# One layer of a hybrid backbone: where decays, context products, head weights and the last splits are placed

## The chip, the cores and the metric

The kernel runs on one core of a Trainium2 chip. A core has TensorE (PE: matrix products into the accumulation memory PSUM, from a stationary operand that a weight load brings in, PEld), VectorE (DVE), ScalarE (ACT: copies, casts, activation functions), GpSimd (POOL) and SyncE (SP: starts transfers). The engines run side by side; each takes its own instructions in order, and semaphores tie them together. The metric is the device time of one execution in microseconds (us). The kernel before takes 1752.54 us, the median of three runs (1750.49 to 1753.95).

## The reference

One layer of a diffusion backbone over 1024 latent tokens (a 16 x 64 grid) and 256 context tokens, of width 1024, all in fp32:

```python
hx = _modulate(_rmsnorm(x, norm1_g[l]), sh1, sc1)        # shifts and scales from c @ w_ada
hc = _modulate(_rmsnorm(ctx, norm1_g[l]), csh1, csc1)
... = jnp.split(hx @ w_in[l], IN_OFFSETS, axis=-1)       # q, k, v of both branches, gates
o_na = _na_latent(grid(xq), grid(xk), grid(xv), kc_na, vc_na, na_rpb[l])
o_ret_c, s_f, s_b = _bi_retention(qc_r, kc_r, vc_r, lg_f, lg_b, s_zero, s_zero)
o_ret_x, _, _ = _bi_retention(q_r, k_r, _heads(xrv, RET_HEADS), lg_f, lg_b, s_f, s_b)
o_ret = _ret_output(o_ret_x, xrg)
x = x + g1 * _merge(o_na, o_ret, xga, xgb, w_proj_na[l], w_proj_ret[l], w_out[l])
x = x + g2 * _conv_ffn(hx2, w_up[l], conv_w[l], conv_b[l], w_down[l])
return _rmsnorm(x, final_norm_g)
```

`_na_latent` is neighbourhood attention (8 heads of 64, window 8 x 16) over local keys and all context keys in one softmax. `_bi_retention` is a chunked linear recurrence in both directions (4 heads, chunks of 128, a log decay `lg` for each head and direction). Its decays inside a chunk are `exp(lg * (pos + 1))`, `exp(lg * (L - 1 - pos))`, and for a whole chunk `exp(lg * L)`; they depend on the position and the head alone.

## The kernel before, in words

**Arithmetic.** Each fp32 operand of a large product is split into a high part, which ScalarE makes with a cast (L88), and a low part, which VectorE makes with a subtraction (L89). Three matmuls, high x high, high x low and low x high, make up one product (`chain` at L105 to L114, `mm3` at L122 to L125, `open3` at L1384 to L1387). A weight tile of 128 x 512 comes by DMA into one of three `raw` buffers (L93), and its split goes into one of six `wc` places, or into a place given by the caller (`wload`). A raw buffer is free for the next load when both halves of its split are done.

**Order.** Each engine's queue follows from when the program is built. Most code is put in order by a program with modelled durations, which takes the earliest written instruction that is ready; it may draw an instruction far ahead of its place in the text if nothing gates it. Code under `tc.manual_schedule()` keeps its written order on every engine, while instructions from outside may be put in between. A tile that reuses memory waits for the readers of the tile that had it before.

**Start (hand-ordered, up to L1010).** Loads, norms, transposes and modulation of the tokens; the products for the first pair of attention heads gather in PSUM tiles `c` (three for each half of the tokens, `first_mm`). At its end stand: `decays(0)` to `decays(3)` (L596 to L604: 24 exponentials of 128 x 1 on ScalarE) and `dec_scale` on POOL (L607); the release of the start's buffers; the evictions `ev_hi` and `ev_lo` of `c` into queries `qS`, keys `kH` and `kL`, and values `vT`; the next pair's query weights, whose second half goes into `place` (ScalarE L635, VectorE L638); products with them (`next_mm`), in the two-buffer PSUM tag `mm`, and their evictions; and last the products of the context tokens with the key and value weights, `ctx_mm(1)` and `ctx_mm(2)`:

```python
    def ctx_mm(t):
        m = mt[0, t, 2] = mm_tile()
        mm_a(m[:, :C], first[t], hcs(0), hcs(1))
```

The SBUF tile `ex`, which holds the exponents of the decays, lies in the start's pool `s0`. PSUM has eight banks. In the start they hold two `tp` and the six `c`; then two go to `mm` and six to the attention's pool `pna` (tags `sl`, `sc`, and `pt` with two buffers).

**Attention.** 32 units (4 pairs of heads x 8 query blocks), each with scores, softmax, transposes and products with the values; further projections fill TensorE between them (`piece`). The ScalarE exponentials are at L484 and L485.

**Retention.** For each head h, `Head(h)` loads eight weight tiles: for head 0 six into `wc` and two into `wx` (six places of their own), for the others 0 to 3 into `wc` and 4 to 7 into `wx`. `front(i)` then makes ten blocks (two of context, eight of the grid) with eight products each, in the order of the weights. `state(i)` makes the running state from `kz` (keys times decay), and the mixing of the head before runs in between.

**Down projection (the end).** Seven products by a Strassen-like scheme, each a sum over eleven weight blocks j, into four PSUM banks for four token blocks. In the last product seven blocks run under `steps(6, ...)`; the last four (`tl`) are split before a hand-ordered part, where TensorE works bank by bank. `finish` (L1938 to L1946) scales a block's output: small POOL operations, one ScalarE and one VectorE instruction, two DMAs from SP. Of the last four blocks of the sixth product, two are finished in the ordered part and two behind the first bank of the hand-ordered part.

Of the kernel before, what the change touches and what calls it, by code (L numbers as in the profile page):

```python
# [8 lines left out]
F32 = mybir.dt.float32  # L9
F32R = mybir.dt.float32r  # L10
AF = mybir.ActivationFunctionType
ALU = mybir.AluOpType
# [4 lines left out]
P = 128  # L17
# [23 lines left out]
def tile_hybrid_layer(ctx, tc: tile.TileContext, io, dbg=None):  # L41
# [24 lines left out]

    cpool = sb("const", "left")
    edge = sb("edge", "right")
    tick = cpool.tile([P, 24], F32, name="pad")[:, 0:1]
    edge.tile([P, 24], F32, name="pad")  # L70

    def const(name, shape):
# [26 lines left out]
    def wload(src, lo_eng=None, into=None):  # L99
        raw = rawload(src)  # L100
        wc = into if into is not None else wtile()
        split(wc[:, 0], wc[:, 1], raw, lo_eng)
        return wc
# [18 lines left out]
    def mm3(out, ah, al, bh, bl, first, last):  # L122
        pe.matmul(out, ah, bh, start=first, stop=False)  # L123
        pe.matmul(out, ah, bl, start=False, stop=False)  # L124
        pe.matmul(out, al, bh, start=False, stop=last)  # L125
# [218 lines left out]
    def mm_tile():  # L344
        return pmm.tile([P, 512], F32, tag="mm", bufs=2, name="mm")
# [184 lines left out]
    def ada_load():  # L530
        w = na.tile([P, D], F32, tag="aw", bufs=2, name="aw")
        sync.dma_start(w, io["w_ada2"][len(ada2)])
        ada2.append(w)
# [56 lines left out]

    def load_ex():
        cst["lg"] = const("lg", [P, 2, RH])
        cst["ex"] = s0.tile([P, 5], F32, name="ex")
        sync.dma_start(cst["ex"], io["expo"])

    def decays(h):  # L596
        lg, ex = cst["lg"], cst["ex"]
        f, b = lg[:, 0, h : h + 1], lg[:, 1, h : h + 1]
        act.activation(dec[:, h, 0:1], ex[:, 0:1], AF.Exp, scale=f)
        act.activation(dec[:, h, 1:2], ex[:, 1:2], AF.Exp, scale=b)  # L600
        act.activation(dec[:, h, 2:3], ex[:, 2:3], AF.Exp, scale=f)
        act.activation(dec[:, h, 3:4], ex[:, 3:4], AF.Exp, scale=b)
        act.activation(dec[:, h, 4:5], ex[:, 4:5], AF.Exp, scale=f)
        act.activation(dec[:, h, 5:6], ex[:, 4:5], AF.Exp, scale=b)  # L604

    def dec_scale():
        pool.tensor_scalar(dec[:, :, 0:2], dec[:, :, 0:2], RKS, None, ALU.mult)  # L607


    pairs, mt, gens = [], {}, {}  # L610
    blocks = {(0, t): first[t] for t in range(3)}
# [38 lines left out]
        pairs[1].evac_lo(0, half, h, mt[1, 0, half])  # L650

    def ctx_mm(t):
        m = mt[0, t, 2] = mm_tile()
        mm_a(m[:, :C], first[t], hcs(0), hcs(1))


# [1 line left out]
    with tc.manual_schedule():  # L658
# [297 lines left out]
        first_mm(0, 7)  # L956
        ctx_l(6)
        ctx_l(7)
        decays(0)
        decays(1)  # L960
        decays(2)
        decays(3)
        first_mm(1, 7)
        dec_scale()
        next_load(1)
        s0.release()
        na = sb("na", "right")
# [91 lines left out]
    for i in range(NPAIR * NJ + 2):  # L1059
        live = i < NPAIR * NJ  # L1060
        u1 = us[i - 1] if 1 <= i <= NPAIR * NJ else None
        u2 = us[i - 2] if i >= 2 else None
        if i == 0:
            ada_load()
            ada_load()
        for n in (0, 1) if i == 1 else (i,) if 1 < i < 32 else ():
            ada_col2(n)
        if u1:
            if u1.j == 0:
                u1.pair.values()  # L1070
            u1.transp(0)
        piece()
        if u1:
            u1.transp(1)
        if live:
            pair = pairs[i // NJ]
            if i % NJ == 0 and i:
                pair.load_bias()
            us.append(Unit(pair, i % NJ))
            us[i].scores()  # L1080
        if u2:
            u2.output()
        if u1:
            u1.values()
            puts(gate_sums, u1.st[:, 14:15], 1)
        piece()
        piece()
# [26 lines left out]
    class Head:  # L1114
        def __init__(self, h):
            self.h = h
            fwd = h % 2 == 0
            self.order = list(range(NTB)) if fwd else list(range(NTB - 1, -1, -1))
            self.back = self.order[::-1]
            self.ci = 0 if fwd else 1  # L1120
            self.oi = 1 - self.ci
            self.wr = []
            for kb in range(KB):
                t = rt.tile([P, 2, 512], F32R, tag="wx", bufs=6, name="wx") if kb >= (KH if h else 6) else None
                self.wr.append(wload(io["w_ret"][h, kb], into=t))
            self.init = [rt.tile([P, DV], F32, tag=f"init{i}", bufs=2, name=f"init{i}") for i in range(2)]
            self.v, self.qk, self.sts, self.dss, self.r0 = {}, {}, {}, {}, {}
            self.sts[self.order[0]] = self.init[self.ci]
            self.run = self.init[self.oi]
            self.o, self.A, self.Q = {}, {}, {}  # L1130
# [4 lines left out]
        def front(self, i):  # L1135

            src, tb = (hcp, i) if i < NCB else (hxp, self.order[i - NCB])
            c0 = P if i < NCB else 0
            m = mm_tile()
            for kb in range(KB):  # L1140
                xh, xl = src(0, kb, tb * P, P), src(1, kb, tb * P, P)
                w = self.wr[kb]
                mm3(m[:, c0:512], xh, xl, w[:, 0, c0:512], w[:, 1, c0:512], kb == 0, kb == KB - 1)
                if kb in (2, 5):
                    yield
            vtag = f"c{i}" if i < NCB else tb
            self.v[i] = v = rt.tile([P, 2, DV], F32R, tag=f"v{vtag}", bufs=1, name="v")
            act.copy(v[:, 0], m[:, 256:512])
            vec.tensor_tensor(v[:, 1], m[:, 256:512], v[:, 0].bitcast(F32), ALU.subtract)
            r0 = rt.tile([P, 2, 2, 2, 32], F32, tag="r0", bufs=2, name="r0")  # L1150
            self.r0[i] = r0f = r0.rearrange("p q a t i -> p q (a t i)")
            if i < NCB:
                act.copy(r0f[:, 1], m[:, P : 2 * P])
                return
            r1 = rt.tile([P, 2, 2, 2, 32], F32, tag="r1", bufs=2, name="r1")
            mv = m[:, 0:256].rearrange("p (q a t i) -> p q a t i", q=2, a=2, t=2)
            for a, ti in ((0, tb), (1, NTB)):
                cs = cosT[:, ti, 0].unsqueeze(1).unsqueeze(1).to_broadcast([P, 2, 2, 32])
# [756 lines left out]
    def gs(dh):  # L1915
        return slice(dh * 512, dh * 512 + 512)
# [21 lines left out]
    def finish(tb, dh):  # L1938
        s, ts = ssf[:, tb], slice(tb * P, (tb + 1) * P)
        pool.tensor_scalar(s[:, 3:4], s[:, dh : dh + 1], 1.0 / D, s[:, 2:3], ALU.mult, ALU.add)  # L1940
        pool.tensor_tensor(s[:, 4:5], s[:, 3:4], mhalf[:, 0:1], ALU.pow)
        z0, z1 = part[tb, 1 - dh], part[tb, dh]
        act.activation(z0, z0, AF.Copy, scale=s[:, 4:5])
        vec.scalar_tensor_tensor(z1, z1, s[:, 4:5], fg[:, gs(dh)], ALU.mult, ALU.mult)
        sync.dma_start(io["out"][ts, gs(1 - dh)], z0)
        sync.dma_start(io["out"][ts, gs(dh)], z1)  # L1946

    stream = Stream([(j, c) for p in DOWN for j in range(NH) for c in p], 8)
# [37 lines left out]
    for b in range(QB):  # L1986
        tb = QB + b
        x, z = rows_of(tb, 0), dw_tile("z", 6)
        part[tb, 0] = z
        vec.tensor_tensor(z, u2[b], banks[1][b], ALU.subtract)  # L1990
        pool.tensor_tensor(z, z, gate2[:, gs(0)], ALU.mult)
        pool.tensor_tensor(z, z, x, ALU.add)
        square(tb, 0, x)
        if b < QB - 2:
            finish(tb, 0)

    steps(6, range(NH - NL), False, False)
    tl = [operands(6, j) for j in range(NH - NL, NH)]
    with tc.manual_schedule():
        for b in range(QB):  # L2000
            ts = slice(b * P, (b + 1) * P)
            for i, (a, w) in enumerate(tl):
                open3(banks[0][b], a[:, 0, ts], a[:, 1, ts], w[:, 0], w[:, 1], False, i == NL - 1)
            if b == 0:
                for tb in (NTB - 2, NTB - 1):
                    finish(tb, 0)
            z, junk = dw_tile("z", 6), dw_tile("xr", 4)
            part[b, 1] = z
            vec.tensor_tensor(z, banks[0][b], gate2[:, gs(1)], ALU.mult)
            vec.tensor_tensor(z, p1[b], z, ALU.subtract)  # L2010
            square(b, 1, junk)
            if b:
                finish(b - 1, 1)
        finish(QB - 1, 1)
# [110 lines left out]
```

## Time and profile before

| what | us |
|---|---|
| three runs, median (lowest to highest) | 1752.54 (1750.49 to 1753.95) |
| the profiled execution, its own time | 1753.51 |
| its span in the profile | 1751.7 |
| VectorE busy, of the span | 1224.6 |
| ScalarE busy, of the span | 852.3 |
| TensorE busy from 112 to 383 (attention) | 270.58 of 271 |

The profile shows one execution. Times count from the start of its span. A row of the timeline gives the start, the duration, the engine (SPq is SP's queue of transfers), the line of the kernel, the operation, what is written from what, and the shapes; x2 at its end means that two such instructions follow each other, and brackets give the idle time of the engine before it and what ended it. A row of the table of stretches gives the length, then the busy time and number of instructions of PE, PEld, DVE, ACT and POOL, then the granted TensorE clock as a share of full speed, the busy share of the DMA engines and their GB/s. The end of a matmul is modelled, so matmuls overlap in the rows; their starts tell the pace.

### The profile page before, as it was taken

How to read it: one execution, taken by the hardware profiler on the slowest of the kernel's cores; microseconds unless marked ns; L12 is line 12 of the kernel's file. 1: busy time of each engine (PE TensorE's matmuls, PEld its weight loads, DVE VectorE, ACT ScalarE, POOL GpSimd, SP SyncE). 2: the span in 40 equal slices, each digit the busy share in tenths (PEclk: the TensorE clock that was granted, in tenths of full speed). 3: DMA queues.
4: the chain of work that ended last, by engine and by line, in shares of the span. 5: the costliest groups of instructions: out<-in, count | busy, mean ns of one | idle time of the engine just before them, and what ended most of it. 6: DMA issues, size and time to landing. Idle time of an engine off the chain costs nothing.

```text
span 1751.7 us, 25084 instructions
## 1 busy us (share of the span) xinstructions
PE 1724.2 (98%) x8405; PEld 1426.8 (81%) x8405; DVE 1224.6 (70%) x2454; ACT 852.3 (49%) x1826; POOL 537.6 (31%) x703
## 2 busy tenths in 40 slices
PE   8999999999999999999999999999999999999997
PEld 4688888888888888888888888788888888888886
DVE  4777788765776766765554556876888889856755
ACT  5666666653443534553444323544444444545444
POOL 1000001002333344513222211012566657421444
PEclk9999999999999999999999999999999999999999
DMA  9144455541322313578876666767666676998754
GB/s 345 63 152 148 126 145 160 177 119 35 103 71 62 88 40 97 159 250 271 272 228 235 194 198 191 253 218 224 189 182 169 188 199 173 256 315 289 242 162 162
DMA packets 141362, 313.02 MB, mean 179 GB/s; under 512 B 19025, under 2 KB 31473, under 8 KB 135025
## 3 DMA queue, kind: packets, MB, share of 16 engines
q1 hardware_dynamic: 117040, 230.66, 39.1%
q0 software_dynamic: 12032, 70.27, 18.0%
q10 hardware_dynamic: 12160, 10.49, 1.8%
q8 instruction: 66, 1.08, 0.3%
q14 instruction: 64, 0.52, 0.1%
HBM read 250.78 MB, written 121.91 MB: 213 GB/s over the span
## 4 chain that ended last, share of the span: by engine, by line
PE 50%; issue 6%; DVE 4%; DMA 4%; POOL 4%; ACT 2%; SPq 0%; POOLq 0%; ACTq 0%; DVEq 0%
PE u L1387 28%; PE pr L114 2%; PE pr L112 2%; PE pr L113 2%; DMA ur<-d_a 2%; PE mm L125 1%; PE mm L123 1%; PE mm L124 1%; PE om L125 1%; PE om L123 1%; PE om L124 1%; DMA d_a<-at 1%; PE pn L113 1%; PE pn L112 1%; PE pn L114 1%
## 5 line engine op out<-in xcount | busy, mean ns | idle before, releaser
L1387 PE MATMUL u<-T,wc 128*128 128x512 f32 x960 | 225.1, 390 | 0.5 <-ACT pu L1421 0.4
L1387 PE MATMUL y<-wc,ahl 128*128 128x512 f32 x924 | 210.4, 389 | 2.1 <-DVE wc L89 2.1
L1387 PEld LDWEIGHTS u<-T,wc 128*128 128x128 f32 x960 | 179.6, 188 | 40.1 <-ACT pu L1421 2.7
L1387 PEld LDWEIGHTS y<-wc,ahl 128*128 128x128 f32 x924 | 173.3, 188 | 38.9 <-DVE wc L89 2.9
L89 DVE TENSOR_TENSOR wc<-ur,wc 128x512 fp32r<-128x512 f32 x161 | 117.1, 730 | 60.2 <-ACT wc L88 58.3
L88 ACT CAST wc<-ur 128x512 fp32r<-128x512 f32 x161 | 99.8, 622 | 118.8 <-PE u L1387 71.4
L113 PE MATMUL mm<-low,wc 128*128 128x512 f32 (+1 forms) x328 | 124.8, 381 | 0.0
L1387 PE MATMUL u<-h2a,wc 128*128 128x512 f32 x480 | 112.8, 390 | 0.1
L112 PE MATMUL mm<-hx,wc 128*128 128x512 f32 x264 | 107.5, 407 | 0.2 <-ACT wc L635 0.2
L1387 PEld LDWEIGHTS u<-h2a,wc 128*128 128x128 f32 x480 | 89.9, 188 | 19.7 <-issue 0.8
L114 PE MATMUL mm<-hx,wc 128*128 128x512 f32 x264 | 105.7, 400 | 0.0
L1387 PE MATMUL u<-hxT,wc 128*128 128x512 f32 x384 | 89.6, 389 | 0.0
L584 POOL COPY pad<-pu 128x1 f32<-128x1 f32 x54 | 36.9, 683 | 160.1 <-DVE pu L1424 117.0
L1387 PEld LDWEIGHTS u<-hxT,wc 128*128 128x128 f32 x384 | 72.1, 188 | 15.0
L584 POOL COPY pad<-st 128x1 f32<-128x1 f32 x32 | 5.9, 185 | 250.7 <-DVE st L487 250.7
L89 DVE TENSOR_TENSOR wc<-raw,wc 128x512 fp32r<-128x512 f32 x86 | 61.9, 722 | 17.3 <-ACT wc L88 17.3
L88 ACT CAST wc<-raw 128x512 fp32r<-128x512 f32 x86 | 53.1, 623 | 39.4 <-PE u L1387 7.4
L88 ACT CAST wc<-s 128x512 fp32r<-128x512 f32 x56 | 34.9, 624 | 69.9 <-PE u L1387 67.7
L125 PE MATMUL mm<-wc,low 128*128 128x512 f32 (+1 forms) x180 | 68.5, 381 | 0.0
L113 PEld LDWEIGHTS mm<-low,wc 128*128 128x128 f32 x328 | 62.9, 192 | 6.8
L1182 ACT ACTIVATE kz<-r,dec 128x128 fp32r<-128x128 f32 x72 | 27.8, 402 | 71.9 <-POOL r L1163 71.5
L1387 PE MATMUL u<-hx,wc 128*128 128x512 f32 x192 | 62.0, 390 | 0.0
(407 smaller groups left out, 4763.4 us busy)
## 6 DMA issues: line engine op xcount, KB each, us to landing
d_a<-at SPq DMA_DIRECT2D x77, 256.0 KB, 5.6
ur<-d_a SPq DMA_DIRECT2D x77, 256.0 KB, 5.3
ur<-in_w_up SPq DMA_DIRECT2D x74, 256.0 KB, 6.7
d_w<-in_w_down POOLq DMA_DIRECT2D x66, 256.0 KB, 7.2
aw<-in_w_ada SPq DMA_DIRECT2D x32, 512.0 KB, 4.1
d_a<-d_a POOLq DMA_DIRECT2D x44, 256.0 KB, 7.5
ur<-d_w SPq DMA_DIRECT2D x44, 256.0 KB, 3.9
d_s<-in_w_up POOLq DMA_DIRECT2D x36, 256.0 KB, 6.1
```

The source lines that it names most:

```text
L88: act.copy(hi, src)
L89: (lo_eng or vec).tensor_tensor(lo, src, hi.bitcast(F32), ALU.subtract)
L112: pe.matmul(out, wh, xh, start=k == 0, stop=False)
L113: pe.matmul(out, wh, xl, start=False, stop=False)
L114: pe.matmul(out, wl, xh, start=False, stop=k == n - 1)
L123: pe.matmul(out, ah, bh, start=first, stop=False)
L124: pe.matmul(out, ah, bl, start=False, stop=False)
L125: pe.matmul(out, al, bh, start=False, stop=last)
L584: late(pool.tensor_copy(tick, src))
L1182: act.activation(kz[:, d, 0], k, AF.Copy, scale=self.dec(d))
L1387: pe.matmul(out, a, b, start=first and n == 0, stop=last and n == 2, skip_group_check=True)
```

## The change

Four edits. (1) The 24 exponentials become six multiplications of `lg` by a column of `ex` on VectorE, each for all heads, and one exponential over the whole of `dec` on ScalarE; they and the scaling on POOL are called in the attention's loop, at unit 8. `ex` moves to the constant pool, whose padding tile shrinks from 24 to 16 columns. (2) The context products go into the attention's `pt` banks. (3) Heads 1 to 3 begin each block with weights 4 to 7 and end with 0 to 3, and the weights are loaded in an order that goes with that. (4) The splits of the last four blocks of the down projection move into the hand-ordered part; three blocks instead of two are finished behind its first bank; the last block's first output goes out from ScalarE's queue.

```diff
-    tick = cpool.tile([P, 24], F32, name="pad")[:, 0:1]
+    tick = cpool.tile([P, 16], F32, name="pad")[:, 0:1]
+    ex = cpool.tile([P, 5], F32, name="ex")
...
-        cst["ex"] = s0.tile([P, 5], F32, name="ex")
-        sync.dma_start(cst["ex"], io["expo"])
-
-    def decays(h):
-        lg, ex = cst["lg"], cst["ex"]
-        f, b = lg[:, 0, h : h + 1], lg[:, 1, h : h + 1]
-        act.activation(dec[:, h, 0:1], ex[:, 0:1], AF.Exp, scale=f)
...
-    def dec_scale():
+        sync.dma_start(ex, io["expo"])
+
+    def decays():
+        for k, e in enumerate((0, 1, 2, 3, 4, 4)):
+            vec.tensor_scalar(dec[:, :, k], lg[:, k % 2], ex[:, e : e + 1], None, ALU.mult)
+        act.activation(dec, dec, AF.Exp)
         pool.tensor_scalar(dec[:, :, 0:2], dec[:, :, 0:2], RKS, None, ALU.mult)
...
     def ctx_mm(t):
-        m = mt[0, t, 2] = mm_tile()
+        m = mt[0, t, 2] = pna.tile([P, 512], F32, tag="pt", bufs=2, name="cm")
         mm_a(m[:, :C], first[t], hcs(0), hcs(1))
...
-        decays(0)
-        decays(1)
-        decays(2)
-        decays(3)
         first_mm(1, 7)
-        dec_scale()
         next_load(1)
...
+        if i == 8:
+            decays()
...
-            self.wr = []
-            for kb in range(KB):
+            self.kbs = (*range(KH, KB), *range(KH)) if h else range(KB)
+            self.wr = {}
+            for kb in (4, 5, 0, 1, 6, 7, 2, 3) if h > 1 else self.kbs:
                 t = rt.tile([P, 2, 512], F32R, tag="wx", bufs=6, name="wx") if kb >= (KH if h else 6) else None
-                self.wr.append(wload(io["w_ret"][h, kb], into=t))
+                self.wr[kb] = wload(io["w_ret"][h, kb], into=t)
...
-            for kb in range(KB):
+            for n, kb in enumerate(self.kbs):
...
-                mm3(m[:, c0:512], xh, xl, w[:, 0, c0:512], w[:, 1, c0:512], kb == 0, kb == KB - 1)
-                if kb in (2, 5):
+                mm3(m[:, c0:512], xh, xl, w[:, 0, c0:512], w[:, 1, c0:512], n == 0, n == KB - 1)
+                if n in (2, 5):
                     yield
...
-        sync.dma_start(io["out"][ts, gs(1 - dh)], z0)
+        (act if tb == QB - 1 else sync).dma_start(io["out"][ts, gs(1 - dh)], z0)
...
-        if b < QB - 2:
+        if b == 0:
             finish(tb, 0)
...
-    tl = [operands(6, j) for j in range(NH - NL, NH)]
     with tc.manual_schedule():
+        tl = [operands(6, j) for j in range(NH - NL, NH)]
...
-                for tb in (NTB - 2, NTB - 1):
+                for tb in range(NTB - 3, NTB):
                     finish(tb, 0)
```

More of the change, by code (lines that the diff above doesn't have):

```diff
@@ L592, in load_ex @@
         cst["lg"] = const("lg", [P, 2, RH])
-        cst["ex"] = s0.tile([P, 5], F32, name="ex")
-        sync.dma_start(cst["ex"], io["expo"])
-    def decays(h):
-        lg, ex = cst["lg"], cst["ex"]
-        f, b = lg[:, 0, h : h + 1], lg[:, 1, h : h + 1]
[L599 to L604, printed above, removed]
-    def dec_scale():
+        sync.dma_start(ex, io["expo"])
[3 more added lines that the diff above has]
+        act.activation(dec, dec, AF.Exp)
         pool.tensor_scalar(dec[:, :, 0:2], dec[:, :, 0:2], RKS, None, ALU.mult)
```

## The prediction

> **What bounds the kernel now.** I read the page first, then the table of who waited for whom on the tensor engine (columns: engine and what waited, what released it, total us, times, longest).
>
> ```profile
> span 1751.7 us, 25084 instructions
> PE 1724.2 (98%) x8405; PEld 1426.8 (81%) x8405; DVE 1224.6 (70%) x2454; ACT 852.3 (49%) x1826; POOL 537.6 (31%) x703
> ```
>
> ```profile
> PE tp L279 <- ACT ccol L241: 4.5, 1, 4.5
> PE tp L279 <- DMA x<-in_w_ada1g: 2.3, 1, 2.3
> PE mm L112 <- DVE qS L417: 2.1, 1, 2.1
> PE y L1387 <- DVE wc L89: 2.1, 2, 1.7
> PE mm L112 <- ACT place L635: 1.4, 1, 1.4
> PE dS L125 <- DVE kz L1183: 1.3, 2, 0.9
> ```
>
> TensorE is busy for 1724.2 of 1751.7 us, so it sets the end, and no edit here takes a matmul away. What can be won is idle time of TensorE and the time in which it runs slowly. The first two waits (6.8 us) belong to the first loads, which stay. The other four are at three places, and each lies where one of the four edits works: the hand-ordered start (2.1 and 1.4), the border between retention heads (1.3), the last matmuls (1.7 of the 2.1). Anything saved there moves everything behind it, because TensorE is nearly always busy in between.
>
> **The start: exponentials and context products.** Timeline rows (start, duration, engine, line, what) of ScalarE and VectorE:
>
> ```profile
> 79.21 1.28 ACT L599 ACT_TABLE_LOAD   x1
> ...
> 84.79 0.30 ACT L604 ACTIVATE dec<-ex,lg 128x1 f32<-128x1 f32 x1
> ...
> 85.48 0.59 ACT L407 CAST kH<-c 64x512 fp32r<-64x512 f32 x1
> 85.96 0.63 ACT L635 CAST place<-raw 128x512 fp32r<-128x512 f32 x1
> ```
>
> ```profile
> 79.83 0.76 DVE L229 TENSOR_TENSOR low<-vc,hc 128x256 fp32r<-128x256 f32 x2
> ...
> 92.07 0.68 DVE L419 TENSOR_TENSOR kL<-c,kH 64x512 fp32r<-64x512 f32 x1
> ...
> 93.38 2.82 DVE L417 SCALAR_TENSOR_TENSOR qS<-mm,qS 64x512 fp32r<-64x512 f32 x4
> ```
>
> and of TensorE over the same time, with the granted clock (the column behind the busy times) in two stretches:
>
> ```profile
> 84.87 0.39 PE L114 MATMUL mm<-hx,wc 128*128 128x512 f32 x1
> 86.65 0.50 PE L112 MATMUL mm<-hx,place 128*128 128x512 f32 x1 [1.39 <-ACT place L635]
> ...
> 88.13 0.39 PE L113 MATMUL mm<-low,place 128*128 128x512 f32 x1
> ...
> 92.45 0.39 PE L114 MATMUL mm<-hx,place 128*128 128x512 f32 x1
> 94.92 0.35 PE L112 MATMUL mm<-hc,wc 128*128 128x256 f32 x1 [2.08 <-DVE qS L417]
> ...
> 96.30 0.28 PE L114 MATMUL mm<-hc,wc 128*128 128x256 f32 x1
> ...
> 102.23 0.40 PE L112 MATMUL mm<-hx,wc 128*128 128x512 f32 x1
> ```
>
> ```profile
> 96.40:99.80 3.40, 3.40 (x18) 3.40 (x17) 0.69 (x1) 1.21 (x3) 0.00 (x0) 0.51 0.23 51
> 99.80:102.20 2.40, 2.40 (x21) 2.40 (x21) 2.00 (x4) 1.39 (x3) 0.00 (x0) 0.98 0.78 173
> ```
>
> The table load and the 24 exponentials hold ScalarE from 79.21 to 85.09, nearly 5.9 us, in front of the evictions and of the cast of `place`, for which TensorE then waits 1.39 us. Without them the evictions can start when the last readers of the start buffers are through, at 79.83 + 0.76 = 80.6 instead of 85.48: 4.9 us earlier. `place` is then cast by 82 and subtracted by 83, ahead of TensorE's need at 85.1 by some 2 us. **Place term:** its 24 matmuls start at 85.1 and not at 86.65. In steady flow they follow each other by (92.45 - 88.13)/19 = 0.227 us, so they end at 85.1 + 24 x 0.227 = 90.6.
>
> The context products then need a bank. Today they take one of the two `mm` banks and wait for the four query evictions at 93.38 (2.08 us). In the attention's `pt` banks they wait only for what last used those banks in the start, the evictions of `c`. These ended at 92.07 + 0.68 = 92.75, and 4.9 earlier is 87.9, before 90.6. **Context term:** 48 matmuls at (96.30 - 94.92)/11 = 0.125 us are 6.0 us at most, so the next product starts at 96.6 at the latest where it started at 102.23.
>
> That is 5.7 us, more than the two waits (3.5 us). Of the rest, 1.6 us is the clock: from 96.40 to 99.80 TensorE ran at 0.51 of its clock, so 3.40 us did the work of 1.74. I charge that to the gap of 2.08 us just before it (behind it, at 99.80, the clock is back at 0.98), and take the whole of it as won. If the slow stretch stayed, the term would be 4.1. The Trainium skill ("TensorE: Matmul & The Clock Gate", HAM oscillation) warns only of idle gaps over some 3.4 us. By that rule a gap of 2.08 us would not halve the clock, the slow stretch would have another cause and could stay, and the sum below would be 1.6 smaller; the row, with the drop right behind the gap, speaks for the gap.
>
> What the start's edit adds elsewhere: one table load, six VectorE multiplications on 128x4, one exponential on 128x24, and the scaling on POOL, which moves along. The prices and covers come from the first unit of the attention and from the attention as a whole:
>
> ```profile
> 108.29 0.51 ACT L484 ACTIVATE P<-P,st 128x256 f32<-128x256 f32 x1 [4.97 <-DVE st L482]
> ```
>
> ```profile
> L482 DVE TENSOR_SCALAR st<-st x32: 149/166/171, 108.1 to 380.1; 128x2 f32<-128x2 f32 x32
> ```
>
> ```profile
> 112.00:383.00 271.00, 270.58 (x1671) 235.40 (x1670) 211.99 (x606) 176.74 (x528) 25.35 (x65) 1.00 0.50 147
> ```
>
> The table load now belongs to the attention's first exponential. ScalarE sat idle for 4.97 us before that, so 1.28 us fits; without that cover it would delay the first unit by 1.28 at most. The Trainium skill ("ScalarE: Activation LUTs", What ACT_TABLE_LOAD costs) prices a switch at 2.66 us with a drain; the load here lasts 1.28, and 2.66 would fit into 4.97 too. The six multiplications cost about 6 x 0.17 = 1.0 us of VectorE, which is busy for 212 of 271 us there, while TensorE is busy for 270.58: I take nothing. Both ends: 0, or 1.0 + 0.3 us of delay if TensorE had to wait for all of it. The results are first used by retention, far behind. The ordering program may also draw them forward into the start, since nothing gates them once `ex` and `lg` are loaded; then 1.28 + 0.3 us come back on ScalarE there. The padding tile gives up the space that `ex` takes, so no other tile moves.
>
> **The heads.** Two context blocks and their states open each head, here head 1 and head 2 in the same stretch (to the first grid block), with the rows of head 1's weights:
>
> ```profile
> 445.93:460.32 14.39, 12.40 (x67) 10.53 (x66) 11.36 (x27) 8.30 (x22) 5.30 (x8) 1.00 0.59 181
> 523.13:534.08 10.95, 10.95 (x70) 10.79 (x68) 7.07 (x21) 5.55 (x15) 3.58 (x6) 1.00 0.61 167
> ```
>
> ```profile
> 447.05 1.25 ACT L88 CAST wx<-raw 128x512 fp32r<-128x512 f32 x2 [1.02 <-DMA raw<-in_w_ret]
> ```
>
> ```profile
> 448.05 2.55 DVE L89 TENSOR_TENSOR wx<-raw,wx 128x512 fp32r<-128x512 f32 x3
> ```
>
> Head 2's opening has no idle time. Head 1's takes 3.44 us longer, with 14.39 - 12.40 = 2.0 us idle. Its `wx` weights have free places, but they are split only here, because the three raw buffers are held by weights 0 to 3, whose `wc` places head 0 frees in its last block. The splits also push back the `kz` subtraction for which TensorE waits (1.3 in the waits). With weights 4 to 7 loaded first they are split during head 0, and weights 0 to 3 are wanted 12 matmuls later. Bounds: 0 (the order comes out as before) to 3.4; the idle alone is 2.0; I take 2.6. Heads 2 and 3 get the same two-ring order with nothing idle to win: 0. The number of loads does not change, and their place in SP's queue moves only among themselves.
>
> **The end.** VectorE, TensorE, then SP at the last output:
>
> ```profile
> 1720.94 1.79 DVE L1944 SCALAR_TENSOR_TENSOR z<-z,ssf,fg 128x512 f32<-128x512 f32 x1 [4.45 <-POOL ssf L1941]
> ...
> 1727.93 0.75 DVE L1944 SCALAR_TENSOR_TENSOR z<-z,ssf,fg 128x512 f32<-128x512 f32 x1 [0.80 <-POOL ssf L1941]
> 1728.60 0.69 DVE L89 TENSOR_TENSOR wc<-ur,wc 128x512 fp32r<-128x512 f32 x1
> ```
>
> ```profile
> 1729.34 13.67 PE L1387 MATMUL y<-wc,ahl 128*128 128x512 f32 x59 [1.66 <-DVE wc L89]
> ```
>
> ```profile
> 1747.07 0.33 SPq L1945 DMA_DIRECT2D out_dram<-x  x1
> 1747.49 0.40 SPq L1946 DMA_DIRECT2D out_dram<-z  x1
> ```
>
> Four finishing multiplications stand ahead of the last splits in VectorE's queue and wait for POOL's small operations; TensorE idles 1.66 us behind them. With the splits written ahead, and three of the four finishes behind the first bank, the splits run in VectorE's idle time: 1.66 us won. The first finish, with its wait of 4.45 us, stays in front but ends at 1722.7, 5 us before TensorE runs dry. The finishes' own outputs leave a bank later, with SP free until the next bank's outputs. The last two outputs go out on two queues, so the second is issued 0.42 us earlier: 0.4 at most, 0 at least. **End term:** 1.7 + 0.4 = 2.1, between 0 and 2.1.
>
> **Sum.** 5.7 + 2.6 + 2.1 = 10.4 us. The profiled execution took 1753.5 us (1.8 around its span), 1.0 above the median of the three. 1753.5 - 10.4 = 1743.1; on the scale of the median 1742.1. I predict **1742 us**.
>
> **Rivals.** First, only part arrives: the clock stays slow (5.7 becomes 4.1), the heads give back their idle alone or nothing, the end only its wait. With 4.1 + 0 to 2.0 + 0 to 1.7 that is 4.1 to 7.8 us, about 1746.5. For it: the waits at the heads are small and scattered. Against it: each release in the rows above is the very thing that an edit moves.
>
> Second, the change does not do what it says: outside the hand-ordered parts the queue order is computed when the program is built, so the exponential may be drawn back into the start, its 1.6 us ahead of the evictions, the head's weights may keep their order, and the finishes may again stand ahead of the splits. Then little is left: about 1751, no difference that can be told (0.2%, 3.5 us, is what a measurement of this kernel can tell).
>
> Third, slower: that same ordering places the attention anew, since its start shifts and six VectorE operations enter at unit 8. One mechanism: in each of the 32 units, a transposed block waits for one VectorE subtraction that is now queued ahead of it (0.69 us by the split's row at the end). 32 x 0.69 = 22 us, less 10.4, gives 1764. It decides from (10.4 + 3.5)/32 = 0.43 us a unit. For it: VectorE is 78% busy in that stage (212 of 271). Against it: TensorE lost only 0.42 us there (271 - 270.58), with filler work in every unit.
>
> **Chances.** All three places deliver (8 to 12 us): 0.55. Only part: 0.25. Nothing that can be told: 0.08. Slower: 0.12. So faster by over 0.2% 0.80, within it 0.08, slower 0.12. The range 1738 to 1750 holds the first two and the edge of the third, and leaves out the slower case, most of the third and the tails: 2 in 10.
>
> **What would show it.** Start: no wait of TensorE on `place` or on `qS`; context products on a tile `cm`, about 90.6, with a granted clock of 1.00 up to the first unit; the next product near 96.5; no `dec` rows before the evictions. Heads: head 1's `wx` splits well before 440, its opening near 11 us without idle. End: no wait of `y` on `wc` near 1720, and the span ending about 8.7 us behind the last matmul as now, less 0.4. The prediction is wrong if the slow clock appears without the gap, if a new wait on `pt` or on the context keys' copy shows up, if the attention has more than 5 us of idle TensorE, or if VectorE's finishes still precede the splits.

## The result, and the profile after

| | us, median (lowest to highest) | runs |
|---|---|---|
| before | 1752.15 (1750.49 to 1753.95) | 4 |
| after | 1742.73 (1741.73 to 1745.6) | 4 |

The ratio is 0.9949, with a 95% interval of 0.9931 to 0.9966; by the medians it is 9.4 us faster. The profiled execution of the new kernel took 1742.64 us by its own time. Its page and the waits of TensorE (engine and what waited, what released it, total us, times, longest):

```profile
span 1740.9 us, 25068 instructions
PE 1721.2 (99%) x8405; PEld 1426.1 (82%) x8405; DVE 1225.3 (70%) x2460; ACT 846.9 (49%) x1803; POOL 537.9 (31%) x703
```

```profile
PE tp L280 <- ACT ccol L242: 4.5, 1, 4.5
PE tp L280 <- DMA x<-in_w_ada1g: 1.9, 1, 1.9
PE Q L125 <- POOL SS L1204: 1.1, 2, 0.9
PE mm L124 <- ACT r L1143: 0.6, 1, 0.6
PE y L1377 <- DVE wc L90: 0.4, 1, 0.4
...
PE sl L475 <- DMA kH<-kH: 0.3, 1, 0.3
```

The waits on `place`, `qS` and `kz` are gone, and of the wait of `y` only a 0.4 is left. New is a wait of `Q` on `SS`, 0.9 us long (another of 0.3 was there before); it counts below. TensorE has 8405 matmuls in both, as many between these moments, so the first matmul of each stage shows where time was gained (starts from the timelines; a gain is before less after):

| first matmul of | before | after | gained so far |
|---|---|---|---|
| the products after the first pair | 79.24 | 79.43 | -0.2 |
| the products with `place` | 86.65 | 85.30 | 1.4 |
| the context products | 94.92 | 90.74 | 4.2 |
| the next product behind them | 102.23 | 96.49 | 5.7 |
| retention (head 0) | 383.35 | 378.86 | 4.5 |
| head 1 | 445.93 | 441.45 | 4.5 |
| head 1's first grid block | 460.32 | 452.21 | 8.1 |
| head 3 | 597.85 | 589.09 | 8.8 |
| the stage behind retention | 719.14 | 712.10 | 7.0 |
| the up projection's main part | 1100.86 | 1093.74 | 7.1 |
| the down projection | 1522.22 | 1513.59 | 8.6 |
| end of the last matmul | 1743.01 | 1732.38 | 10.6 |
| end of the span | 1751.72 | 1740.87 | 10.8 |

**Start.** TensorE's timeline, then the stretches behind the context products (length, busy time of PE, PEld, DVE, ACT and POOL, then the granted clock), then VectorE and ScalarE:

```profile
79.43 0.50 PE L113 MATMUL mm<-hx,wc 128*128 128x512 f32 x1 [0.16 <-ACT wc L627]
...
85.30 0.39 PE L113 MATMUL mm<-hx,place 128*128 128x512 f32 x1
...
90.74 0.28 PE L113 MATMUL cm<-hc,wc 128*128 128x256 f32 x1
...
96.49 0.40 PE L113 MATMUL mm<-hx,wc 128*128 128x512 f32 x1
```

```profile
90.00:93.40 3.40, 3.40 (x27) 3.24 (x27) 2.05 (x4) 1.80 (x3) 0.00 (x0) 1.00 0.11 42
93.40:96.80 3.40, 3.40 (x30) 3.36 (x29) 2.90 (x6) 2.08 (x5) 0.00 (x0) 1.00 0.48 130
```

```profile
89.45 1.39 DVE L418 SCALAR_TENSOR_TENSOR qS<-mm,qS 64x512 fp32r<-64x512 f32 x2 [1.25 <-ACT qS L404]
92.17 1.39 DVE L418 SCALAR_TENSOR_TENSOR qS<-mm,qS 64x512 fp32r<-64x512 f32 x2 [1.32 <-ACT qS L404]
```

```profile
54.95 1.28 ACT L599 ACT_TABLE_LOAD   x1
56.24 0.22 ACT L599 ACTIVATE dec<-dec 128x24 f32<-128x24 f32 x1
```

No idle time stands ahead of `place` or of the context products, and the clock is 1.00 throughout. The query evictions now run in two pairs, at 89.45 and 92.17, where all four stood in one row at 93.38. The exponential is not in the attention: the ordering program drew it forward to 56.24, some 24 us ahead of the first eviction (`kH`, at 79.80).

**Heads.** The `wx` splits on VectorE as one group (shortest, median, longest in ns, then first and last start), and the openings of heads 1 and 2:

```profile
L90 DVE TENSOR_TENSOR wx<-raw,wx x6: 681/682/693, 385.5 to 395.0; 128x512 fp32r<-128x512 f32 x6
```

```profile
441.45:452.21 10.76, 10.76 (x68) 10.60 (x66) 8.93 (x23) 7.12 (x19) 5.23 (x8) 1.00 0.64 192
515.17:526.14 10.97, 10.97 (x69) 10.82 (x68) 8.41 (x24) 7.14 (x19) 5.34 (x8) 1.00 0.72 219
```

Two of the six splits belong to head 0 and four to head 1. So head 1's own-ring weights are split by 396, during head 0, and its opening has no idle time.

**End.** VectorE, TensorE, and the queues of the last outputs:

```profile
1712.64 1.78 DVE L1934 SCALAR_TENSOR_TENSOR z<-z,ssf,fg 128x512 f32<-128x512 f32 x1 [4.46 <-POOL ssf L1931]
...
1721.84 0.68 DVE L90 TENSOR_TENSOR wc<-ur,wc 128x512 fp32r<-128x512 f32 x1
1722.44 2.07 DVE L1934 SCALAR_TENSOR_TENSOR z<-z,ssf,fg 128x512 f32<-128x512 f32 x3
```

```profile
1714.77 17.61 PE L1377 MATMUL y<-wc,ahl 128*128 128x512 f32 x77
```

```profile
1735.72 1.08 SPq L1936 DMA_DIRECT2D out_dram<-z  x2
1736.44 0.40 ACTq L1935 DMA_DIRECT2D out_dram<-x  x1
```

The last three finishes follow behind the last split, and TensorE runs from 1714.77 to its end without a gap.

### The profile page after: what moved, and what is told of

Same layout as the page of the kernel before. It is cut to its first block, busy times and chain, and to the rows that moved or that the text cites. A ratio compares the mean times of both kernels' runs of the same rounds, so it can differ in the third digit from the quotient of the medians.

```text
span 1740.9 us, 25068 instructions
## 1 busy us (share of the span) xinstructions
PE 1721.2 (99%) x8405; PEld 1426.1 (82%) x8405; DVE 1225.3 (70%) x2460; ACT 846.9 (49%) x1803; POOL 537.9 (31%) x703
## 4 chain that ended last, share of the span: by engine, by line
PE 81%; DMA 5%; issue 5%; DVE 4%; POOL 3%; ACT 2%; SPq 0%; POOLq 0%; ACTq 0%; DVEq 0%
PE u L1377 29%; PE mm L126 4%; PE mm L124 4%; PE mm L125 4%; PE mm L115 3%; PE mm L113 3%; PE mm L114 3%; PE y L1377 2%; PE R L514 2%; PE om L125 2%; PE om L124 2%; PE om L126 2%; PE pr L114 2%; PE pr L113 2%; PE pr L115 2%
## 5 line engine op out<-in xcount | busy, mean ns | idle before, releaser
L114 PE MATMUL mm<-low,wc 128*128 128x512 f32 (+1 forms) x312 | 119.1, 382 | 0.0
L114 PEld LDWEIGHTS mm<-low,wc 128*128 128x128 f32 x312 | 58.9, 189 | 7.1
L89 ACT CAST wc<-wr 128x512 fp32r<-128x512 f32 x56 | 34.7, 622 | 56.3 <-PE u L1377 47.2
```

The lines of the kernel that those rows point to most:

```text
L89: act.copy(hi, src)
L114: pe.matmul(out, wh, xl, start=False, stop=False)
```

## The experiments

A comparison on one chip has its own runs of the kernel before; their medians were 1752.10, 1752.65 and 1753.63 in the three sets.

**The four edits one at a time.** Each is one of the four, put into the kernel before. The first:

```diff
-    def decays(h):
...
+        if i == 8:
+            decays()
```

> The kernel before with the decays edit alone. Theory (each release works where its rows lie): the wait of TensorE on place is gone and its 24 matmuls start 1.3 to 1.6 us earlier, at about 85.2; the context products still wait for the query evictions behind them, about 2 us, because those follow the place matmuls and not the exponentials. If the slow clock behind the context products comes from the gap just before them, the stretch of about 3.4 us at 0.51 stays; the next product after them then starts 1.5 to 2.1 us earlier than before. Rival (the slow clock comes from the two gaps together, 1.39 and 2.08 us): the slow stretch goes with the first gap and the next product starts about 3.5 us earlier. Time: 1.5 to 3.5 us less than before.

The second:

```diff
-        m = mt[0, t, 2] = mm_tile()
+        m = mt[0, t, 2] = pna.tile([P, 512], F32, tag="pt", bufs=2, name="cm")
```

> The kernel before with the context products in the pt banks alone. Theory: the wait on place (1.39 us) stays, since the 24 exponentials still hold ScalarE; the wait on qS (2.08 us) is gone unless the pt banks are evicted late (VectorE ends these at 92.75 in the kernel before, just as the products come up), the clock stays at 1.00 and the next product starts about 3.5 to 4 us earlier. Rival (the first gap alone slows the clock, or the pt banks come free late): the slow stretch stays and the gain is 2 us or less.

The third:

```diff
-            for kb in range(KB):
+            self.kbs = (*range(KH, KB), *range(KH)) if h else range(KB)
...
+            for kb in (4, 5, 0, 1, 6, 7, 2, 3) if h > 1 else self.kbs:
```

> The kernel before with the order of the head weights alone. Theory: the opening of head 1 shrinks from 14.39 us to about 10.8, the openings of heads 2 and 3 stay at about 10.9, and everything before head 1 is unmoved; gain 3 to 3.6 us. Rival (the gain seen with all four edits came from the shifted start and another order of the queues, not from the weights): the opening of head 1 stays above 13 us.

The fourth:

```diff
-    tl = [operands(6, j) for j in range(NH - NL, NH)]
     with tc.manual_schedule():
+        tl = [operands(6, j) for j in range(NH - NL, NH)]
...
-        if b < QB - 2:
+        if b == 0:
```

> The kernel before with the three edits of the end alone (splits in the hand-ordered part, three finishes behind the first bank, the last output's first half from ScalarE's queue). Theory: no wait of y on wc near 1727, last matmul about 1.7 us earlier, the end 2.0 us earlier, nothing before 1690 moved by more than some tenths. Rival (the gap only moves, to the first bank's eviction or the finishes): the last matmul is less than 0.5 us earlier.

| alone | median (lowest to highest) | ratio, 95% interval |
|---|---|---|
| decays | 1750.57 (1748.84 to 1752.46) | 0.9988 (0.9979 to 0.9998) |
| context | 1751.03 (1749.55 to 1753.09) | 0.9994 (0.9985 to 1.0004) |
| heads | 1750.85 (1746.68 to 1752.11) | 0.9989 (0.9979 to 0.9998) |
| end | 1750.49 (1746.4 to 1751.61) | 0.9988 (0.9979 to 0.9997) |

By their medians the four save 1.5, 1.1, 1.2 and 1.6 us, 5.5 in all. Each interval is about 1.7 us to either side, so the totals can't price the edits; the traces can. For the start, I count from the first product after the first pair, because that moment itself wanders by 2 us between executions (78.6 to 80.7 in those of this text):

| us after that product | `place` | context products | next product |
|---|---|---|---|
| before | 7.41 | 15.68 | 22.99 |
| decays alone | 5.85 | 11.54 | 17.37 |
| context alone | 7.37 | 13.41 | 19.16 |
| end alone (start as before) | 7.37 | 15.64 | 22.94 |
| heads alone (start as before) | 7.37 | 15.63 | 21.46 |
| after | 5.87 | 11.31 | 17.06 |

The decays alone bring 5.6 of the 5.9 us: both waits and the slow clock are gone. I had expected the wait on `qS` to stay; that fell. The context edit alone brings 3.8, but the wait on `place` is left, and behind it TensorE, now early, meets the copy of the context keys (timeline of TensorE, context alone):

```profile
87.40 0.50 PE L112 MATMUL mm<-hx,place 128*128 128x512 f32 x1 [1.37 <-ACT place L635]
...
102.41 0.36 PE L474 MATMUL sl<-kH,qS 128*128 128x256 f32 x1 [0.99 <-DMA kH<-kH]
```

With the heads alone the opening of head 1 gains 3.63 us (1.37 us ahead at its start, 5.00 at its first grid block), and from head 3 to the stage behind retention 2.2 are lost again (5.64 to 3.48). With the end alone the last matmul ends 3.23 us earlier, but 1.20 of that was there at the down projection's first matmul, so the edit's part is 2.0, and the output adds 0.24.

**The clock.** Two of these kernels have the start of before, and their slow stretch in different places. Heads alone, a row of TensorE and then stretches:

```profile
86.78 0.50 PE L112 MATMUL mm<-hx,place 128*128 128x512 f32 x1 [1.36 <-ACT place L635]
```

```profile
88.00:90.00 2.00, 2.00 (x7) 1.56 (x6) 1.92 (x4) 1.95 (x4) 1.63 (x2) 0.66 0.85 186
90.00:92.00 2.00, 2.00 (x6) 1.52 (x5) 1.74 (x3) 1.97 (x5) 0.00 (x0) 0.50 1.00 396
92.00:94.00 2.00, 2.00 (x10) 1.61 (x10) 1.94 (x4) 1.42 (x3) 0.00 (x0) 0.99 0.40 162
```

Here the clock fell some 2 us behind the end of the first gap. It slowed TensorE while the query evictions caught up, so that the second gap shrank to 0.4, and nothing slow came after it. That is why its next product came 1.5 us sooner than before's. With the end alone it fell behind the second gap, as in before:

```profile
94.63 0.35 PE L112 MATMUL mm<-hc,wc 128*128 128x256 f32 x1 [2.06 <-DVE qS L417]
```

```profile
96.00:99.40 3.40, 3.40 (x19) 3.40 (x19) 0.69 (x1) 0.75 (x2) 0.00 (x0) 0.55 0.02 1
```

With the context alone, which has only the first gap, of 1.37 us, ending at 87.40, nothing slow came behind it:

```profile
90.00:92.00 2.00, 2.00 (x10) 1.65 (x9) 1.72 (x3) 1.95 (x5) 0.31 (x1) 1.00 0.98 351
```

The kernels of the end's two parts, further below, also have the start of before. Both went the way of the heads alone: a first gap of 1.38 and 1.39 us, half the clock from 90 to 92, a second gap of 0.4, and the next product 21.5 us behind the first product after the first pair. So of five executions with this start, two took 22.9 to 23.0 us for it and three took 21.5. The gain of 5.9 us in the table is against one of the slower two; against the other three it is 4.4 (21.46 less 17.06). No difference between the kernels says which of the two comes.

Earlier in the start every execution has a gap of 1.8 to 2.8 us that ends some 10 us from the start of the span. A stretch at half the clock followed it in two of the thirteen (before, gap of 2.28 us, and the second execution of the new kernel that comes below, 2.10), and none where the gap was longest (heads alone, 2.77). So the length of a gap alone does not decide.

**Are the `pt` banks needed?** The new kernel, with the context products back in an `mm` bank:

```diff
-        m = mt[0, t, 2] = pna.tile([P, 512], F32, tag="pt", bufs=2, name="cm")
+        m = mt[0, t, 2] = mm_tile()
```

> The changed kernel with the context products back in the mm banks. Theory (the wait on qS was also made by the 24 exponentials; in the run with the decays edit alone the context products did not wait): no wait on qS, full clock behind, the next product at about 96.5 as in the changed kernel, the same time within 1 us. Rival (my prediction: the pt banks remove that wait): TensorE waits about 2 us before the context products, with or without the slow clock.

It took 1744.35 us (1743.4 to 1747.29), ratio to before 0.996 (0.9946 to 0.9973). TensorE shows no wait at the context products, and VectorE shows why:

```profile
90.16 0.36 PE L113 MATMUL mm<-hc,wc 128*128 128x256 f32 x1
```

```profile
88.62 1.39 DVE L418 SCALAR_TENSOR_TENSOR qS<-mm,qS 64x512 fp32r<-64x512 f32 x2 [1.26 <-ACT qS L404]
91.34 1.39 DVE L418 SCALAR_TENSOR_TENSOR qS<-mm,qS 64x512 fp32r<-64x512 f32 x2 [1.33 <-ACT qS L404]
```

The first `mm` bank is read out by 90.01, just before the context products want it at 90.16. The wait on `qS` had been a late eviction, not a missing bank. With the decays gone from there, the second edit is worth 0.3 us: the next product starts 17.35 us behind the first product after the first pair here (95.99 less 78.63), and 17.06 in the new kernel.

**Decays where the text has them.** The new kernel, with the multiplications and the exponential pinned to their place in unit 8:

```diff
-            vec.tensor_scalar(dec[:, :, k], lg[:, k % 2], ex[:, e : e + 1], None, ALU.mult)
-        act.activation(dec, dec, AF.Exp)
+            late(vec.tensor_scalar(dec[:, :, k], lg[:, k % 2], ex[:, e : e + 1], None, ALU.mult))
+        late(act.activation(dec, dec, AF.Exp))
```

> The changed kernel with the six multiplications and the exponential held at their written place (unit 8), where the changed kernel's queues had drawn them into the start (VectorE 52.8 to 53.5, table load at 54.95). Theory (they cost nothing in the start, where both engines have idle time, and nothing in the attention): table load before the attention's first exponential at 103, inside its idle time; the same time within 1 us, milestones within 0.5. Rival (pulled forward they cost up to 1.6 us there, or at unit 8 they hold back TensorE): one of the two shows over 1 us at the unit or in the start.

1745.39 us (1744.22 to 1745.73), ratio 0.9958 (0.9945 to 0.997). ScalarE loads the table for the attention's first exponential, in idle time:

```profile
99.05 1.28 ACT L485 ACT_TABLE_LOAD   x1
104.09 0.51 ACT L485 ACTIVATE P<-P,st 128x256 f32<-128x256 f32 x1 [3.76 <-DVE st L483]
```

So the load costs nothing there, but the attention came out in another order; its longest new gap on TensorE is

```profile
118.63 0.55 PE L496 MATMUL ptp<-ident,P 128*128 128x128 f32 x3 [0.77 <-ACT P L485]
```

It lies ahead of the decays, which run at 169.5 to 171. At the end of the attention this kernel had gained 2.92 us against before, the new kernel 4.49; 0.92 of the difference was there at the first product after the first pair (80.35 against 79.43), so 0.7 us is the price of the pinned place, where I had expected 0.5 at most.

**The same program again, and head 3.** Once the new kernel unchanged, and once with another order of the weights in the last head alone:

> The changed kernel once more, beside the kernel before on one chip. The four edits alone gave medians 1.1 to 1.6 us below the kernel before, 5.5 together; the changed kernel gave 9.4. Theory (the edits are nearly independent, and the 9.4 came partly from a kernel before that was measured a little high and four runs of the changed kernel): 6 to 9 us less than before. Rival (the edits need each other): 9 to 11 us less.

```diff
-            self.kbs = (*range(KH, KB), *range(KH)) if h else range(KB)
+            self.kbs = range(KB) if not h else (4, 5, 0, 1, 2, 3, 6, 7) if h == RH - 1 else (*range(KH, KB), *range(KH))
```

> The changed kernel, but head 3 takes its weights in the order 4 5 0 1 2 3 6 7 in each block, so that its last block frees the wc places of 0 to 3 earlier (they are what the gate weights behind it wait for). Theory (the 1.7 us given back between head 3 and the end of retention come from the gate weights splitting 3 us later, so that less filler stands before POOL's sum and its subtraction): first gate split some 1 to 1.5 us earlier against the last block's end, wait of Q on SS under 0.5 us, 1 to 1.7 us less by the end of retention. Rival (POOL's transfer chain alone sets that wait): Q still waits 0.8 us or more, same time.

The program again: 1745.0 us (1744.32 to 1745.1), ratio 0.9956 (0.9943 to 0.9968). The other order: 1742.8 (1740.74 to 1743.46), ratio 0.9942 (0.993 to 0.9955). The intervals overlap, so the totals leave it open whether the order helps. In the traces it does. In the new kernel, POOL and TensorE in head 3:

```profile
666.39 0.81 POOL L553 DMA_DIRECT2D d_g<-d_g  x1
...
671.34 0.78 POOL L553 DMA_DIRECT2D d_g<-d_g  x1 [3.12 <-DMA d_g<-d_g]
671.91 0.98 POOL L1204 TENSOR_TENSOR SS<-st,SS 128x256 fp32r<-128x256 f32 x1
```

```profile
673.62 0.50 PE L125 MATMUL Q<-SS,qk 128*128 128x512 f32 x1 [0.88 <-POOL SS L1204]
```

and with the other order:

```profile
669.91 0.78 POOL L553 DMA_DIRECT2D d_g<-d_g  x1 [2.99 <-DMA d_g<-d_g]
670.48 0.99 POOL L1204 TENSOR_TENSOR SS<-st,SS 128x256 fp32r<-128x256 f32 x1
```

```profile
672.19 0.50 PE L125 MATMUL Q<-SS,qk 128*128 128x512 f32 x1 [0.19 <-POOL SS L1204]
```

POOL waits 3 us for one transfer of the gate weights before it can issue the next, and the `SS` subtraction stands behind it in POOL's queue. That wait is in both, and the kernel before has it too (2.78 us, at 678.35) without idle time of TensorE behind it; what differs is how much work TensorE has in hand when it comes. With weights 0 to 3 last in each block of head 3, their `wc` places come free late: the first gate weight is cast into one at 659.99, 70.9 us behind the head's start, where before had it at 665.44, 67.6 behind; with the other order it is at 658.50, 69.7 behind. That this is how the order comes to the wait is argued, not shown. That the order sets the wait is shown: in the new kernel, its second execution and the two variants above with the same order it is 0.7 to 1.1 us, with the other order here and in the last experiment 0.2 and 0.3. From head 3's start to the end of retention the new kernel loses 1.7 us against before, 0.9 of it in that wait; the other order loses 0.6.

The repeat also shows how much one execution can wander. Both executions were alike to within 0.8 us up to the up projection, but that stage, from the up projection's first matmul to its last, the same ones in the same order, took

```profile
1093.74:1523.20 429.46, 428.72 (x1888) 352.30 (x1887) 359.61 (x424) 204.20 (x295) 207.21 (x215) 1.00 0.71 207
```

in the first, and in the second

```profile
1093.00:1525.80 432.80, 430.63 (x1888) 351.90 (x1887) 363.09 (x424) 204.23 (x295) 207.18 (x215) 1.00 0.72 205
```

with before's at 431.0 and the other kernels' between 430.1 and 432.1. So the 1.5 us that the table above shows between 1093 and 1514 lie within this wandering and can't be put down to the change.

**The end's two parts.** The kernel before, first with the splits moved alone, then with the three finishes alone:

```diff
-    tl = [operands(6, j) for j in range(NH - NL, NH)]
     with tc.manual_schedule():
+        tl = [operands(6, j) for j in range(NH - NL, NH)]
```

> The kernel before with the four last splits written into the hand-ordered part, and nothing else of the end. Theory (what counts is that the splits stand ahead of the finishing multiplications in VectorE's queue, and of the four finishes only those of the hand-ordered part, the third and fourth, came wrongly ahead): the wait near 1727 is gone or under 0.5 us, the last matmul 1.2 us or more earlier. Rival (the finish of the second block, left in the ordered part, still holds VectorE for POOL): the wait stays over 1 us.

```diff
-        if b < QB - 2:
+        if b == 0:
...
-                for tb in (NTB - 2, NTB - 1):
+                for tb in range(NTB - 3, NTB):
```

> The kernel before with three finishes instead of two behind the first bank, and the splits left outside the hand-ordered part. Theory (finishes written in the hand-ordered part are queued at once, ahead of splits that are still waiting their turn): the wait of y on wc near 1727 stays, 1.2 us or more. Rival (the second finish was the one that held VectorE): the wait falls under 0.5 us.

A single time each, 1750.51 and 1752.38 us; TensorE's gap of 1.66 us shrank to 0.21 with the first,

```profile
1726.37 5.96 PE L1387 MATMUL y<-wc,ahl 128*128 128x512 f32 x25 [0.21 <-DVE wc L89]
```

and with the second it was gone. From the down projection's first matmul to its last, the first gained 1.5 us (2.98 less 1.45) and the second 1.6 (1.14 and 0.48 that it was behind); both together 2.0. With the three finishes alone VectorE shows

```profile
1725.40 0.76 DVE L1944 SCALAR_TENSOR_TENSOR z<-z,ssf,fg 128x512 f32<-128x512 f32 x1 [1.84 <-POOL ssf L1941]
1726.61 0.76 DVE L1944 SCALAR_TENSOR_TENSOR z<-z,ssf,fg 128x512 f32<-128x512 f32 x1 [0.45 <-POOL ssf L1941]
1727.29 0.68 DVE L89 TENSOR_TENSOR wc<-ur,wc 128x512 fp32r<-128x512 f32 x1
```

The needed split still stands behind finishes that wait for POOL, but behind three, not four, and it ends before TensorE is through with what it has. I had held that only the splits' new place could remove the gap; that fell. Either part alone takes away the gap, or all but 0.2 us of it, and brings 1.5 or 1.6 of the 2.0 us. Each of these numbers is from one execution.

**Both simplifications.** The new kernel with the other order of head 3 and the context products back in `mm`:

```diff
-        m = mt[0, t, 2] = pna.tile([P, 512], F32, tag="pt", bufs=2, name="cm")
+        m = mt[0, t, 2] = mm_tile()
...
-            self.kbs = (*range(KH, KB), *range(KH)) if h else range(KB)
+            self.kbs = range(KB) if not h else (4, 5, 0, 1, 2, 3, 6, 7) if h == RH - 1 else (*range(KH, KB), *range(KH))
```

> The changed kernel with head 3's own order of weights (4 5 0 1 2 3 6 7) and the context products back in the mm banks. Theory: both hold together, no wait of TensorE on qS, none over 0.3 us on the context keys' copy or on SS; about 1 us less than the changed kernel, near 1743, ratio 0.993 to 0.996, with about 1 us of luck in the up projection either way. Rival (the two shift each other's queues): back at the changed kernel's time or above.

1743.21 us (1741.23 to 1745.84), ratio 0.9946 (0.9933 to 0.9958): as fast as the new kernel as far as this tells, with one edit less, and not shown to be faster.

## Why the prediction was right

The forecast was 1742 and the median came out at 1742.73. The sum was 10.4 us and the two spans differ by 10.8, of which 1.5 may be the wandering of one stage. Point by point:

**Start: 5.7 forecast, 5.9 found, with one step wrong and some luck.** The next product was to start at 96.6 at the latest and started at 96.49; `place` was to come 1.55 earlier and came 1.54 (7.41 less 5.87), and the clock was to bring 1.6 and brought 1.56 (what the start gained behind the first context product: 7.31 less 5.75). The step that failed is the context term, "In the attention's `pt` banks they wait only for what last used those banks": it gave the 2.1 us and the clock to the second edit. The decays alone bring them. The prediction worked out that the evictions start 4.9 us earlier (the first came 5.7 earlier, at 79.80, and did not wait for the subtraction that was to hold it up to 80.6), used it for `place` and for the evictions of `c`, and did not carry it on to the four query evictions at 93.38, which stand in the same queues. The sum came out right because both edits were made. The luck is in the profiled execution of before: it was one of the two with the slower start, and against the other three the same start gains 4.4. Which of the two the timed runs of before had isn't known.

**The slow clock belonged to the gaps.** It is in all five executions that have both gaps, and in none of the seven that have neither. The prediction charged it to the second gap; in three of the five it stands behind the first. The Trainium skill ("TensorE: Matmul & The Clock Gate", HAM oscillation) warns only of gaps over some 3.4 us. Here gaps of 1.36 and 2.06 us stood ahead of a clock of 0.50 to 0.55, so the measurement decides against the rule as a safe bound. But not every such gap does it, as the 1.37 us of the context edit alone and the 2.77 us near 10 in the heads alone show.

**Attention: forecast as costing nothing, cost 1.2.** Of the 5.7 us, 4.5 arrive at retention. The forecast's first half, that the exponential might be drawn forward, is what happened, at no visible cost: "no `dec` rows before the evictions" was a wrong sign to look for. The same 1726 matmuls took longer (before, after, and the context edit alone, whose window catches one more at its border):

```profile
102.23:383.35 281.12, 280.70 (x1726) 244.09 (x1725) 216.12 (x618) 181.66 (x542) 26.24 (x66) 1.00 0.50 146
96.49:378.86 282.37, 281.67 (x1726) 244.44 (x1725) 216.92 (x618) 181.69 (x542) 26.20 (x66) 1.00 0.49 146
99.19:381.44 282.25, 280.78 (x1727) 244.05 (x1725) 216.49 (x618) 181.35 (x542) 26.12 (x66) 1.00 0.51 147
```

The context edit alone keeps before's order of TensorE there and loses 1.1 us, nearly all in its wait of 0.99 on the copy of the context keys, which TensorE now reaches early. In the new kernel that wait is 0.3. The rest of its loss comes with another order of the same matmuls, most of it in busy and not in idle time; which step of that order costs it is open. A new wait on the keys' copy was one of the prediction's signs of being wrong, so that sign came up, at 0.3 us. The slower rival decided from 0.43 us a unit; 1.2 us over 32 units are 0.04.

**Heads: 2.6 forecast, 2.6 found, by another sum.** Head 1's opening was the mechanism described, and its gain 3.6 us (14.39 to 10.76), a little over the upper bound of 3.4. Then 0.8 came during head 2, of which 0.5 was idle time of TensorE that went, and 1.7 were lost from head 3 on, so retention ends 2.6 further ahead than it began (7.04 less 4.49). That both sums are 2.6 is luck. The step that failed is "Heads 2 and 3 get the same two-ring order with nothing idle to win: 0". It holds for head 2's opening (10.95 and 10.97), not for the rest of head 2, and head 3 hands its `wc` places to the gate weights, and these came late (the wait is shown to follow the order, the way between them is argued). The prediction priced the weights' order for the head that reads them and not for the stage that inherits their places.

**End: 2.1 forecast, 2.2 found.** The last matmuls gained 2.0, the output 0.2 of its 0.4 at most. Splits before finishes, the first finish in front, no wait: as written. That the edit was built of two parts that each remove the gap was not seen.

**The total.** The start brought 5.9, 1.2 of it was lost again in the attention, the heads brought 2.6 and the end 2.2: 9.5, beside 1.5 of the up projection and small change. With the quicker start of before it would be 8.0. By the totals it is 9.4 us in the first comparison and 7.7 in the repeat (1752.65 less 1745.0). The sum of 10.4 was 1 to 2.5 too much, by the attention's loss and the form of before's start. The repeat's 7.7 lies just inside the rival "only part arrives" (4.1 to 7.8), so the totals alone don't separate the two; the traces show that all three places delivered.

## What to carry to other kernels

When an engine's block of work is taken out, move its whole queue forward, and every later wait on that queue, before crediting another edit with one of those waits; two edits that cure the same wait are worth it once. When the order of use of a buffer ring changes, ask who gets its places next, beyond the loop that was changed. And where totals differ by a thousandth, compare the first matmul of each stage: it prices an edit to a few tenths of a microsecond where the medians of runs can't. But take it from more than one execution: here the same start took 21.5 or 22.9 us, and one stage 429.5 or 432.8.

## What the runs showed of the hardware

Five executions have a gap of 1.36 to 1.39 us on TensorE at `place` and a second one before the context products. Each has one slow stretch at half the clock, none has it twice: three behind the first gap (2 us after its end with the heads alone), two behind the second. The context edit alone has the first gap, at 1.37 us, and no slow stretch. Of the gaps that end some 10 us into the execution (1.8 to 2.8 us long), two of thirteen were followed by one. What decides it these runs don't show; the length of the gap alone does not. And the table load of 1.28 us was followed by its activation 1.29 us after it began (54.95 and 56.24), with no further pause.
